# A two-layer streaming-encoder trunk on one Trainium2 core: late left operands kept on chip, and four re-ordered streams around the output product of layer 1

## The chip, the cores and the metric

The kernel runs on one core of a Trainium2 chip. A core has a matrix engine (PE, whose weight loads PEld overlap its matmuls), a vector engine (DVE), an activation engine (ACT), GpSimd (POOL) and SyncE (SP), and 16 DMA engines that all queues share. SP and POOL issue this kernel's DMAs here. The metric is the device time of one execution in microseconds (us).

## The reference

Two layers, each on x of 512 frames by 2048 features:

```python
h = rmsnorm(x, g_pre)
z = h @ w_in              # gq, gk, gv, gg, ga, aq, ak, av, ag
o_gla = gated linear attention over chunks of 64 frames, 4 heads (q, k: 128 wide, v: 256)
o_att = chunked softmax attention, 8 heads of 128, own chunk and 8 before it
o_gla = rmsnorm(o_gla, g_gla) * silu(gg);  o_att = rmsnorm(o_att, g_att) * silu(ag)
y = concatenate([o_gla, o_att]) @ w_out
x = x + rmsnorm(y, g_post)
```

Everything is float32; the result is x after the second layer.

## The kernel before

**The products.** Large products (w_in, w_out) are done on pairs of 512-column blocks by a seven-product scheme of Strassen's kind: P1, P5, P6, P3, P7, P2, P4, each a product of a sum of left blocks (S1 for P5, S2 for P6, S4 for P3, S3 for P7, A22 for P4) with a sum of weight blocks. A product is done in four chunks c of the contracted dimension, and one (product, chunk) is a **job**: 12 PE matmuls of 128x512, in fp32 precision built of a high and a low part of both operands: high weights `wh` against high left part, low weights `wl` against high left part, `wh` against low left part. A left operand is a tile of 128x1024 that holds high and low part (tags `sa`, `a...`, `g...`).

**What a job needs.** (1) `raw` (or `H`), 512 KB of weights, loaded by SP (L184, ring of four tiles); (2) for P5 and P6 a weight sum `H<-H,raw` on DVE (L250), for P7 a difference `raw<-H,raw` (L253); (3) the cast `wh` on ACT (L261); (4) the remainder `wl` on DVE (L267, ring of three); (5) the left operand, either resident, or brought back from device memory by SP (L238, in `bring`: `sa<-A`, `sa<-S`, `sa<-oS`).

**The part the change touches** is in layer 1, from about 1340 us on: the last input product (the value pair, GV), then the output product in two pairs of blocks, `W01` and `W23`. While PE does the value pair and the first output pair's P1 and P2, the gated-linear-attention half-heads are finished. `gla_line` runs them as units: outer products (L1300), states on DVE (L1320, L1322), read (PE, L1337), squares for the norm (ACT, L1347), gate (DVE, L1359), and `turn`: transposes on PE (L1370) and an eviction on ACT (L1381). `paired_sums` then makes S1, S2, S4 and S3 (DVE, L1512) and splits each into a high part (ACT cast, L113) and a low part (DVE, L114). The chunks come in the order 2, 3, 0, 1 (`C_END`); the sums of chunks 0 and 1 are the late ones, since they need the last units. S1 and S3 stay on chip. S2 and S4 are written to device memory (`oS`, POOL, L1526) and brought back by SP as `sa` when a job of P6 or P3 wants them, once for each output pair.

**Other streams around it.** `project` takes a finished output block from PE's bank: a sum of squares on ACT (L1598) and a product with the gains on DVE (L1601), the gains being loaded by POOL (L1588). `fetch_operands` (L1542) loads the attention half of the left operand (op_att, four tiles of 512 KB). `load_tokens` (L620) loads rows of the residual stream `x_mid` for the last sum; the half `xs1` is six loads, 2 MB.

**What sets the order.** Each engine works its instructions in order, and so does each DMA queue start its transfers. The order on each engine is set by the tile scheduler from a simulated timeline of the program; `tc.issue_after(x)` puts an instruction behind x, `delayed` and the pump of tasks say how many jobs on a task is called.

Of the kernel before, what the change touches and what calls it, by code (L numbers as in the profile page):

```python
# [35 lines left out]
def hybrid_trunk(  # L36
# [124 lines left out]
    last_evac = [None]  # L161
    last_out, last_put = [None], [None]
    last_cast, last_load, last_low, last_norm, last_state = [None], [None], [None], [None], [None]
# [14 lines left out]
    class Job:  # L178
# [39 lines left out]
        def bring(self):  # L218
# [5 lines left out]
            src = (so_d if end else sa_d)[self.l].get((name, c))  # L224
            if end and self.l in PAIRED and name in ("S1", "S3"):
                return
# [13 lines left out]
        def high(self):  # L240
            k, c, p = self.kind, self.c, self.pair
            if k == "std":
                src = self.raw
            else:
                h, r = p.get(("H", c)), p.get(("r", c))
                src = h if k in ("P1", "P5", "P6", "P4") and h is not None else r
                if k in ("P5", "P6") or k == "P4" and p["early"]:
                    opening = k == "P5" and self.b0 == W01[0]
                    with tc.issue_after(last_out[0]) if opening else nullcontext():
                        nc.vector.tensor_tensor(out=h, in0=h, in1=r, op=ALU.add)  # L250
                elif k == "P7":
                    with tc.issue_after(lows[-2]):
                        nc.vector.tensor_tensor(out=r, in0=h, in1=r, op=ALU.subtract)  # L253
# [170 lines left out]
    class Pair:  # L424
# [60 lines left out]
        def operand(self, job, k, c):  # L485
            if job.a is not None:
                return job.a
            if self.end and self.l in PAIRED and k in ("P5", "P7"):
                until(lambda: (LEFT[k], c) in A)
                return A[LEFT[k], c]  # L490
# [402 lines left out]
    def layer(l):  # L893
# [384 lines left out]
        class Unit:  # L1278
# [64 lines left out]
            def norm(self):  # L1343
                ss, self.r = sm(2), sm(2)
                for tt in range(2):
                    j = t2((256,), BF16)
                    nc.scalar.activation(  # L1347
                        j, self.ps_o[:, tt * 256 : (tt + 1) * 256], AF.Square, scale=256 ** -0.5,
                        accum_out=ss[:, tt : tt + 1],
                    )  # L1350
                if paired:
# [13 lines left out]
            def turn(self):  # L1365
# [13 lines left out]
                for f in range(2):  # L1379
                    kt = 2 * h + f  # L1380
                    nc.scalar.activation(  # L1381
                        full_o[:, f * 256 : (f + 1) * 256], ps[:, f * 256 : (f + 1) * 256], AF.Copy,
                        scale=gcol[:, l * 2 * KT + KT + kt : l * 2 * KT + KT + kt + 1],
                    )
                if paired and p:
# [43 lines left out]
        def gla_line():  # L1429
# [4 lines left out]
            while n < 8 or older is not None:  # L1434
# [25 lines left out]
                if older is not None:  # L1460
                    older.gate()
                    delayed.append([4 if newer is not None else 2, older.turn])
                yield
# [19 lines left out]
        def paired_sums():  # L1483
# [14 lines left out]
            while order:  # L1498
# [24 lines left out]
                if name in ("S1", "S3"):  # L1523
                    A[name, c] = z
                else:
                    last_put[0] = nc.gpsimd.dma_start(so_d[l][name, c], flat(z)).ins  # L1526
                made.add((l, True, name, c))
                yield
# [6 lines left out]
        def fetch_operands(k, c):  # L1535
            passed.add((k, c))
            for i in range(4):
                if ("P7", 1) in passed and 2 * i in heads_done and (0, i) not in op_att:
                    op_att[0, i] = slot(f"a11{i}", [2, 512], F32R)
# [102 lines left out]
        def paired_out():  # L1642
# [14 lines left out]
            def side(n):  # L1657
                def f(k, c):
# [10 lines left out]
                    elif (k, c) == ("P4", C_END[0]):  # L1669
                        gains[n] = load_gain(n, nc.gpsimd)  # L1670
                    if (n, k, c) in ((2, "P5", C_END[3]), (0, "P4", C_END[0])):
                        i = int(n == 0)
                        with tc.issue_after(last_put[0]):
                            held["xs", i] = load_tokens(i, x_src, nc.gpsimd)
                return f
# [141 lines left out]
```

## Time and profile before

| | us |
|---|---|
| median of 3 runs | 1617.53 (1614.9 to 1620.63) |
| the profiled execution's own time | 1618.17 |
| its span on the core | 1616.4 |
| PE busy in the span | 1584.1 (98%) |
| PEld | 1344.4 (83%) |
| DVE | 1274.6 (79%) |
| ACT | 931.7 (58%) |
| POOL | 172.2 (11%) |

A busy PE is not PE at its peak, since matmuls are pipelined and their ends modelled: one 128x512 matmul is listed with 0.39 us, but in an unbroken run the next one starts 0.227 us after it. So what PE loses is read from the rows in which it is idle and from the start times, not from its busy share. The same holds for DVE: a 128x1024 sum is listed with about 1.22 us, and the next instruction starts 1.14 us after it.

### The profile page before, as it was taken

To read this page: it belongs to the slowest core of one execution; us is meant where nothing else is said; L and a number is where in the kernel's file an instruction comes from. 1 tells how busy PE (TensorE), PEld (TensorE's weight loads), DVE (VectorE), ACT (ScalarE), POOL (GpSimd) and SP (SyncE) were. 2 spreads that over 40 slices of the span, in tenths; PEclk is the share of its full clock that TensorE was granted. 3 is DMA by queue.
4 is the path that set the end of the run, shared out by engine and by line. 5 is a ranking of instruction groups with operands and counts; after the bars stand their busy time and mean duration, and the time that the engine had idled before them with its cause. 6 is when DMAs were issued, how large, how long until landed. Compare 5 with 4: busy or idle time off the path is not lost.

```text
span 1616.4 us, 24395 instructions
## 1 busy us (share of the span) xinstructions
PE 1584.1 (98%) x8770; PEld 1344.4 (83%) x8770; DVE 1274.6 (79%) x1590; ACT 931.7 (58%) x1540; POOL 172.2 (11%) x300
## 2 busy tenths in 40 slices
PE   9999999999999999999999999999999999999897
PEld 5787889999988877788878888899999887677675
DVE  6878876877887876688859887868788767768788
ACT  8565544556686544555776555446667665456353
POOL 1131000001001101310121200000010010011101
PEclk9999999999999999999999999999999999999999
DMA  9999966858868697999778998768596757967795
GB/s 373 359 341 334 343 223 241 306 177 307 293 209 287 226 358 245 334 370 331 302 270 329 334 324 296 279 224 287 182 303 224 257 202 270 334 228 276 267 356 178
DMA packets 147753, 459.70 MB, mean 284 GB/s; under 512 B 16188, under 2 KB 35652, under 8 KB 147632
## 3 DMA queue, kind: packets, MB, share of 16 engines
q1 hardware_dynamic: 125936, 383.43, 67.2%
q0 software_dynamic: 21120, 73.76, 12.0%
q8 instruction: 69, 1.13, 0.3%
q10 hardware_dynamic: 576, 0.95, 0.2%
q14 instruction: 52, 0.43, 0.1%
HBM read 392.23 MB, written 64.77 MB: 283 GB/s over the span
## 4 chain that ended last, share of the span: by engine, by line
PE 88%; issue 4%; DVE 3%; DMA 3%; ACT 1%; POOL 0%; SPq 0%; POOLq 0%; DVEq 0%
PE mm L527 52%; PE mm L512 20%; PE mm L398 5%; PE ax L1128 2%; DMA raw<-in_w_dram 2%; DVE wl L267 1%; DMA H<-in_w_dram 1%; PE ax L1111 1%; PE ax L1300 1%; PE ax L1337 1%; DVE H L250 1%; PE ax L527 1%; PE ax L721 1%; PE ax L1090 1%; PE ax L1091 1%
## 5 line engine op out<-in xcount | busy, mean ns | idle before, releaser
L261 ACT CAST wh<-H 128x1024 fp32r<-128x1024 f32 x251 | 263.4, 1052 | 225.7 <-PE mm L527 93.2
L267 DVE TENSOR_TENSOR wl<-raw,wh 128x1024 fp32r<-128x1024 f32 x248 | 302.5, 1220 | 108.6 <-PE mm L527 37.2
L261 ACT CAST wh<-raw 128x1024 fp32r<-128x1024 f32 x248 | 260.9, 1053 | 212.7 <-PE mm L527 94.8
L267 DVE TENSOR_TENSOR wl<-H,wh 128x1024 fp32r<-128x1024 f32 (+1 forms) x253 | 307.2, 1217 | 86.0 <-PE mm L527 33.7
L527 PE MATMUL mm<-wh,sa 128*128 128x512 f32 x1088 | 347.6, 393 | 6.8 <-DMA sa<-oS 3.7
L527 PE MATMUL mm<-wh,g 128*128 128x512 f32 x928 | 289.6, 391 | 0.2 <-ACT mm L551 0.2
L527 PE MATMUL mm<-wh,a 128*128 128x512 f32 x864 | 278.3, 395 | 2.2 <-ACT a L113 1.1
L527 PEld LDWEIGHTS mm<-wh,sa 128*128 128x128 f32 x1088 | 203.2, 188 | 52.5 <-issue 5.2
L512 PE MATMUL mm<-sa,wh 128*128 128x256 f32 x1280 | 236.0, 285 | 0.0
L250 DVE TENSOR_TENSOR H<-H,raw 128x1024 f32<-128x1024 f32 x176 | 213.5, 1220 | 24.2 <-DMA raw<-in_w_dram 14.9
L527 PE MATMUL mm<-wl,sa 128*128 128x512 f32 x544 | 213.1, 392 | 0.1
L527 PEld LDWEIGHTS mm<-wh,g 128*128 128x128 f32 x928 | 174.9, 189 | 36.8 <-ACT mm L551 0.6
L512 PEld LDWEIGHTS mm<-sa,wh 128*128 128x128 f32 x1280 | 199.4, 192 | 0.3
L527 PEld LDWEIGHTS mm<-wh,a 128*128 128x128 f32 x864 | 161.2, 188 | 41.7 <-issue 5.0
L527 PE MATMUL mm<-wl,g 128*128 128x512 f32 x464 | 182.5, 393 | 6.1 <-DVE wl L267 5.9
L512 PE MATMUL mm<-sa,wl 128*128 128x256 f32 x640 | 180.8, 283 | 0.0
L527 PE MATMUL mm<-wl,a 128*128 128x512 f32 x432 | 169.8, 394 | 2.7 <-DVE wl L267 2.7
L512 PEld LDWEIGHTS mm<-sa,wl 128*128 128x128 f32 x640 | 122.3, 191 | 0.1
L527 PEld LDWEIGHTS mm<-wl,sa 128*128 128x128 f32 x544 | 102.2, 188 | 22.2 <-DVE wl L267 1.2
L527 PEld LDWEIGHTS mm<-wl,g 128*128 128x128 f32 x464 | 87.3, 188 | 29.1 <-DVE wl L267 11.2
L527 PEld LDWEIGHTS mm<-wl,a 128*128 128x128 f32 x432 | 81.2, 188 | 22.2 <-DVE wl L267 5.0
L512 PE MATMUL mm<-a,wh 128*128 128x256 f32 x512 | 94.5, 285 | 0.0
(227 smaller groups left out, 2016.3 us busy)
## 6 DMA issues: line engine op xcount, KB each, us to landing
raw<-in_w_dram SPq DMA_DIRECT2D x356, 512.0 KB, 5.3
sa<-S SPq DMA_DIRECT2D x128, 512.0 KB, 4.6
H<-in_w_dram SPq DMA_DIRECT2D x67, 512.0 KB, 6.0
S<-g POOLq DMA_DIRECT2D x32, 512.0 KB, 6.0
g<-S SPq DMA_DIRECT2D x32, 512.0 KB, 5.2
sa<-A SPq DMA_DIRECT2D x32, 512.0 KB, 6.1
sa<-oS SPq DMA_DIRECT2D x32, 512.0 KB, 5.4
oS<-g POOLq DMA_DIRECT2D x24, 512.0 KB, 5.9
```

The lines of the kernel that those rows point to most:

```text
L250: nc.vector.tensor_tensor(out=h, in0=h, in1=r, op=ALU.add)
L261: last_cast[0] = nc.scalar.copy(self.wh, src).ins
L267: last_low[0] = nc.vector.tensor_tensor(out=self.wl[:, kk, :], in0=self.src[:, kk, :], in1=self.wh[:, kk, :].bitcast(F32), op=ALU.subtract ...
L398: mm = nc.tensor.matmul(pss[o], a[:, part, t], rhs[:, kk, :], start=(i == 0 and kk == 0 and m == 0), stop=(i == n - 1 and kk == 1 and m == 2),
L512: nc.tensor.matmul(dst, lhs[:, kk, f], a[:, part, tok], start=(fresh and kk == 0 and m == 0 and ft % 2 == 0), stop=(c == self.last and kk ...
L527: mm = nc.tensor.matmul(out_ps[t], a[:, part, tok], rhs[:, kk, :], start=(fresh and kk == 0 and m == 0), stop=(c == self.last and kk == 1 ...
L721: mm = nc.tensor.matmul(gate_ps[l][g : g + 32, half * 256 : (half + 1) * 256], gate_w[l][:, kh * 8 + c * 2 + kk, :], full[half, c][:, kh, ...
L1090: nc.tensor.matmul(ps[:, :n], self.qh[:, t], self.kl[:, :n], start=False, stop=False)
L1091: nc.tensor.matmul(ps[:, :n], self.ql[:, t], self.kh[:, :n], start=False, stop=True)
L1111: nc.tensor.transpose(ps[:, j * P : (j + 1) * P], self.prob[i][:, j * P : (j + 1) * P], ident)
L1128: nc.tensor.matmul(o, self.pt[i][:, j * P : (j + 1) * P], av[hd // 4, j // 2][:, j % 2, (hd % 4) * P : (hd % 4 + 1) * P], start=(j == 0), ...
L1300: mm = nc.tensor.matmul(self.ps_u[cc][:, tt * 256 : (tt + 1) * 256], kd[p][r, tt, hk], self.gv[p][r, tt, hv], start=True, stop=True,).ins
```

## The change

All five parts act in layer 1 only. (1) The late S2 and S4 (chunks 0 and 1) stay on chip for the first output pair: `paired_sums` still writes them to device memory, since the second pair reads all eight from there, but `bring` returns and `operand` hands the tile itself to P6 and P3. (2) The rule that puts the weight sums of P5 behind `last_out` (the last L1601) holds for the late chunks alone, no longer for chunks 2 and 3. (3) The four op_att loads go to four places of the value pair (P5 chunk 3, P6 chunk 1, P6 chunk 3, P3 chunk 3) and no longer stand together at P7 chunk 1. (4) The newer half-head's squares (L1347) go in front of the older one's eviction (L1381), and the older one's `turn` is called 8 pump steps later and not 4. (5) The six loads of `xs1` are issued by SP without a rule, and no longer by POOL behind the last `oS` write.

```diff
--- before.py
+++ after.py
@@ -159,7 +159,7 @@
     HEAD = (("P1", 0), ("P1", 1), ("P2", 0), ("P2", 1), ("P1", 2), ("P2", 2))
     LEFT = {"P5": "S1", "P6": "S2", "P3": "S4", "P7": "S3", "P4": "A22"}
     last_evac = [None]
-    last_out, last_put = [None], [None]
+    last_out, last_put, last_square = [None], [None], [None]
     last_cast, last_load, last_low, last_norm, last_state = [None], [None], [None], [None], [None]
     made = set()
     lows, casts = [], []
@@ -222,7 +222,7 @@
             if self.a is not None:
                 return
             src = (so_d if end else sa_d)[self.l].get((name, c))
-            if end and self.l in PAIRED and name in ("S1", "S3"):
+            if end and self.l in PAIRED and (name in ("S1", "S3") or not p.get("second") and c in C_END[2:]):
                 return
             if src is None or p.get("direct") or p.get("second") and not end and (name, c) in RESIDENT:
                 return
@@ -245,7 +245,7 @@
                 h, r = p.get(("H", c)), p.get(("r", c))
                 src = h if k in ("P1", "P5", "P6", "P4") and h is not None else r
                 if k in ("P5", "P6") or k == "P4" and p["early"]:
-                    opening = k == "P5" and self.b0 == W01[0]
+                    opening = k == "P5" and self.b0 == W01[0] and c in C_END[2:]
                     with tc.issue_after(last_out[0]) if opening else nullcontext():
                         nc.vector.tensor_tensor(out=h, in0=h, in1=r, op=ALU.add)
                 elif k == "P7":
@@ -485,7 +485,7 @@
         def operand(self, job, k, c):
             if job.a is not None:
                 return job.a
-            if self.end and self.l in PAIRED and k in ("P5", "P7"):
+            if self.end and self.l in PAIRED and k in ("P5", "P6", "P3", "P7"):
                 until(lambda: (LEFT[k], c) in A)
                 return A[LEFT[k], c]
             if k in ("P1", "P2", "P4") and (self.l, LEFT.get(k), c) not in S_on:
@@ -1344,10 +1344,10 @@
                 ss, self.r = sm(2), sm(2)
                 for tt in range(2):
                     j = t2((256,), BF16)
-                    nc.scalar.activation(
+                    last_square[0] = nc.scalar.activation(
                         j, self.ps_o[:, tt * 256 : (tt + 1) * 256], AF.Square, scale=256 ** -0.5,
                         accum_out=ss[:, tt : tt + 1],
-                    )
+                    ).ins
                 if paired:
                     nc.gpsimd.tensor_scalar(out=ss, in0=ss, scalar1=EPS, scalar2=None, op0=ALU.add)
                     last_norm[0] = rsqrt(self.r, ss)
@@ -1378,10 +1378,11 @@
                 full_o = t2()
                 for f in range(2):
                     kt = 2 * h + f
-                    nc.scalar.activation(
-                        full_o[:, f * 256 : (f + 1) * 256], ps[:, f * 256 : (f + 1) * 256], AF.Copy,
-                        scale=gcol[:, l * 2 * KT + KT + kt : l * 2 * KT + KT + kt + 1],
-                    )
+                    with tc.issue_after(last_square[0]) if paired else nullcontext():
+                        nc.scalar.activation(
+                            full_o[:, f * 256 : (f + 1) * 256], ps[:, f * 256 : (f + 1) * 256], AF.Copy,
+                            scale=gcol[:, l * 2 * KT + KT + kt : l * 2 * KT + KT + kt + 1],
+                        )
                 if paired and p:
                     og_full[h] = full_o
                 else:
@@ -1459,7 +1460,7 @@
                     yield
                 if older is not None:
                     older.gate()
-                    delayed.append([4 if newer is not None else 2, older.turn])
+                    delayed.append([8 if newer is not None else 2, older.turn])
                 yield
                 yield
                 older = newer
@@ -1524,6 +1525,8 @@
                     A[name, c] = z
                 else:
                     last_put[0] = nc.gpsimd.dma_start(so_d[l][name, c], flat(z)).ins
+                    if c in late:
+                        A[name, c] = z
                 made.add((l, True, name, c))
                 yield
 
@@ -1535,7 +1538,8 @@
         def fetch_operands(k, c):
             passed.add((k, c))
             for i in range(4):
-                if ("P7", 1) in passed and 2 * i in heads_done and (0, i) not in op_att:
+                free = (("P5", 3), ("P6", 1), ("P6", 3), ("P3", 3))[len(op_att)] if paired and len(op_att) < 4 else ("P7", 1)
+                if free in passed and 2 * i in heads_done and (0, i) not in op_att:
                     op_att[0, i] = slot(f"a11{i}", [2, 512], F32R)
                     src = flat(turned[i][0]) if i == HEADS[-1] // 2 else oa_d[l][0, i]
                     with tc.issue_after(last_load[0]):
@@ -1668,10 +1672,11 @@
                         gains[n + 1] = load_gain(n + 1, nc.gpsimd)
                     elif (k, c) == ("P4", C_END[0]):
                         gains[n] = load_gain(n, nc.gpsimd)
-                    if (n, k, c) in ((2, "P5", C_END[3]), (0, "P4", C_END[0])):
-                        i = int(n == 0)
+                    if (n, k, c) == (2, "P5", C_END[3]):
                         with tc.issue_after(last_put[0]):
-                            held["xs", i] = load_tokens(i, x_src, nc.gpsimd)
+                            held["xs", 0] = load_tokens(0, x_src, nc.gpsimd)
+                    if (n, k, c) == (0, "P4", C_END[0]):
+                        held["xs", 1] = load_tokens(1, x_src, nc.sync)
                 return f
 
             until(lambda: all((0, i) in op_att or fetch_operands("end", 0) for i in range(4)))
```

The order that comes of it shows at three places; in the rows, the number behind a tile's name is its place in the program, and lines after the change count up to four higher (L1601 is then L1605, L1512 is L1513, L1478 is L1479, L1481 is L1482).

The first place is DVE where PE goes from P2 to P5 of the first output pair (wl_14774 is the first `wl` of P5, H_14357 its weight sum, H_14392, H_14431 and the last H those of the three further chunks). Before:

```order
L1601 TENSOR_TENSOR g_2949_14706<-mm_14374,t_2934_14628 128x512
L1601 TENSOR_TENSOR g_2952_14712<-mm_14375,t_2934_14628 128x512
L250 TENSOR_TENSOR H_14357<-H_14357,raw_14702 128x1024
L1512 TENSOR_TENSOR sa_14394<-sa_14394 128x512
L1512 TENSOR_TENSOR t_2897_14457<-a_2957_14735,t_2897_14457 128x512
L1512 TENSOR_TENSOR t_2907_14499<-a_2959_14740,t_2907_14499 128x512
L250 TENSOR_TENSOR H_14392<-H_14392,raw_14733 128x1024
L1512 TENSOR_TENSOR sa_14433<-sa_14433 128x512
L250 TENSOR_TENSOR H_14431<-H_14431,raw_14779 128x1024
L250 TENSOR_TENSOR H_14486<-H_14486,raw_14817 128x1024
L267 TENSOR_TENSOR wl_14774<-H_14357,wh_14731 128x1024
```

With the change:

```order
L250 TENSOR_TENSOR H_14357<-H_14357,raw_14702 128x1024
L267 TENSOR_TENSOR wl_14728<-raw_14684,wh_14700 128x1024
L1605 TENSOR_TENSOR g_2949_14706<-mm_14374,t_2934_14628 128x512
L1605 TENSOR_TENSOR g_2952_14712<-mm_14375,t_2934_14628 128x512
L1513 TENSOR_TENSOR sa_14394<-sa_14394 128x512
L1513 TENSOR_TENSOR t_2905_14489<-a_2957_14735,t_2905_14489 128x512
L1513 TENSOR_TENSOR t_2907_14499<-a_2959_14740,t_2907_14499 128x512
L1513 TENSOR_TENSOR sa_14433<-sa_14433 128x512
L250 TENSOR_TENSOR H_14392<-H_14392,raw_14733 128x1024
L267 TENSOR_TENSOR wl_14774<-H_14357,wh_14731 128x1024
```

H_14357 has moved ahead of both L1605 rows, and two of the four weight sums now come behind wl_14774; between the first L1605 and wl_14774 stand six instructions of 128x512 in both, but one weight sum where there were four.

The second place is SP's queue in the same stretch, ahead of P5's weights (raw_14702 is that of P5's first job). Before:

```order
L184 DMA raw_14622<-in_w_dram 128x1024
L1478 DMA a_2957_14735<-fa_176 128x2x256 x2
L184 DMA raw_14648<-in_w_dram 128x1024
L1481 DMA a_2958_14736<-fg_188 128x512
L184 DMA raw_14666<-in_w_dram 128x1024
L184 DMA raw_14684<-in_w_dram 128x1024
L184 DMA raw_14702<-in_w_dram 128x1024
L184 DMA raw_14733<-in_w_dram 128x1024
```

With the change:

```order
L184 DMA raw_14622<-in_w_dram 128x1024
L620 DMA g_3059_15223<-x_mid 128x1024
L1479 DMA a_2957_14735<-fa_176 128x2x256 x2
L184 DMA raw_14648<-in_w_dram 128x1024
L1482 DMA a_2958_14736<-fg_188 128x512
L620 DMA g_3060_15224<-x_mid 128x1024
L184 DMA raw_14666<-in_w_dram 128x1024
L620 DMA bias_15228<-x_mid 128x512
L184 DMA raw_14684<-in_w_dram 128x1024
L184 DMA raw_14702<-in_w_dram 128x1024
L620 DMA sg_15230<-x_mid 128x512
L184 DMA raw_14733<-in_w_dram 128x1024
```

Four of the six row loads now stand among the weight loads, three of them ahead of raw_14702; the other two stand just ahead of raw_14622.

The third place is DVE at the end of the value pair, at the states that the second half-head's read waits for (H_13473 is a weight sum of the same stretch, raw_14167 or raw_14156 its weights). Before:

```order
L267 TENSOR_TENSOR wl_14203<-H_13443,wh_14199 128x1024
L463 SCALAR_TENSOR_TENSOR g_2846_14212<-mm_13720,norm_210,ev_13873 128x512
L1320 COPY g_2816_14077<-ax_13709 128x256
L250 TENSOR_TENSOR H_13473<-H_13473,raw_14167 128x1024
L1322 SCALAR_TENSOR_TENSOR g_2816_14077<-g_2816_14077,a_end_8127,ax_13710 128x256
L1322 SCALAR_TENSOR_TENSOR g_2816_14077<-g_2816_14077,a_end_8127,ax_13709 128x256
```

With the change:

```order
L250 TENSOR_TENSOR H_13473<-H_13473,raw_14156 128x1024
L463 SCALAR_TENSOR_TENSOR g_2846_14212<-mm_13720,norm_210,ev_13873 128x512
L267 TENSOR_TENSOR wl_14203<-H_13443,wh_14199 128x1024
L1320 COPY g_2820_14085<-ax_13709 128x256
L1322 SCALAR_TENSOR_TENSOR g_2820_14085<-g_2820_14085,a_end_8127,ax_13710 128x256
L1322 SCALAR_TENSOR_TENSOR g_2820_14085<-g_2820_14085,a_end_8127,ax_13709 128x256
```

The weight sum, which waits for its weights, no longer stands between the states; on PE the read itself stands 14 matmuls later among the jobs than before.

## The prediction

> **What bounds the kernel now.** I began with the page's busy times: PE is the bound nearly everywhere.
>
> ```profile
> PE 1584.1 (98%) x8770; PEld 1344.4 (83%) x8770; DVE 1274.6 (79%) x1590; ACT 931.7 (58%) x1540; POOL 172.2 (11%) x300
> ```
>
> So only idle time of PE can be won. The table of what PE waits for, over the stretch from 1395 us to the end, names it (us in total, times, longest):
>
> ```profile
> PE mm L527 <- DVE wl L267: 6.7, 7, 3.3
> PE mm L527 <- DMA sa<-oS: 3.7, 2, 2.3
> PE mm L527 <- DMA sa<-A: 1.7, 1, 1.7
> PE ax L1337 <- DVE g L1322: 1.1, 1, 1.1
> PE mm L527 <- ACT ev L450: 0.9, 2, 0.7
> ```
>
> That is 14 us. Where the largest begins, PE's timeline shows:
>
> ```profile
> 1474.28 0.39 PE L527 MATMUL mm<-wl,a 128*128 128x512 f32 x1
> ...
> 1474.96 0.39 PE L527 MATMUL mm<-wl,a 128*128 128x512 f32 x1
> ...
> 1477.45 0.61 PE L527 MATMUL mm<-wh,g 128*128 128x512 f32 x2
> 1481.34 0.50 PE L527 MATMUL mm<-wl,g 128*128 128x512 f32 x1 [3.28 <-DVE wl L267]
> ```
>
> Three matmuls take 0.68 us, so one takes 0.227 and a job of twelve 2.72 us. At 1477.45 PE enters P5 of the first output pair and stands for 3.28 us. The windows of the next stretches tell whose work that is (columns: us, PE, PEld, DVE, ACT, POOL busy, PE clock, DMA share, GB/s):
>
> ```profile
> 1477.00:1500.00 23.00, 18.15 (x69) 13.52 (x68) 23.00 (x29) 15.81 (x25) 0.31 (x1) 0.93 0.45 165
> 1482.00:1486.00 4.00, 3.96 (x11) 2.62 (x9) 4.00 (x7) 2.93 (x5) 0.00 (x0) 0.57 0.90 362
> ```
>
> DVE is busy for all 23 us of P5, PE is not; behind the 3.28 us wait the clock was 0.57 for 4 us. P5 is bound by DVE, and DVE's timeline shows its order:
>
> ```profile
> 1469.29 1.23 DVE L267 TENSOR_TENSOR wl<-raw,wh 128x1024 fp32r<-128x1024 f32 x1 [1.94 <-PE mm L527]
> ...
> 1471.93 1.28 DVE L1601 TENSOR_TENSOR g<-mm,t 128x512 f32<-128x512 f32 x2
> 1473.12 1.21 DVE L250 TENSOR_TENSOR H<-H,raw 128x1024 f32<-128x1024 f32 x1
> 1474.26 0.68 DVE L1512 TENSOR_TENSOR sa<-sa 128x512 f32<-128x512 f32 x1
> 1474.86 1.28 DVE L1512 TENSOR_TENSOR t<-a,t 128x512 f32<-128x512 f32 x2
> 1476.06 1.22 DVE L250 TENSOR_TENSOR H<-H,raw 128x1024 f32<-128x1024 f32 x1
> 1477.20 0.68 DVE L1512 TENSOR_TENSOR sa<-sa 128x512 f32<-128x512 f32 x1
> 1477.80 2.35 DVE L250 TENSOR_TENSOR H<-H,raw 128x1024 f32<-128x1024 f32 x2
> 1480.07 1.21 DVE L267 TENSOR_TENSOR wl<-H,wh 128x1024 fp32r<-128x1024 f32 x1
> ...
> 1495.24 1.21 DVE L267 TENSOR_TENSOR wl<-H,wh 128x1024 fp32r<-128x1024 f32 x1
> ```
>
> Start to start, a 128x1024 instruction costs 1.14 us (2.27 for the two at 1477.80) and one of 128x512 0.60. From T = 1471.93, the first L1601, to the first remainder of P5 are 9.3 us; four of the eleven instructions are weight sums.
>
> **Late S2 and S4 on chip (part 1).** POOL's and SP's timelines and the chain of waits show the reload:
>
> ```profile
> 1503.17 1.13 POOL L1526 DMA_DIRECT2D oS<-g  x2 [1.20 <-DVE g L114]
> 1504.54 1.05 POOL L620 DMA_DIRECT2D g<-x_mid  x2 [0.24 <-issue]
> ...
> 1506.67 1.11 POOL L620 DMA_DIRECT2D sg<-x_mid  x2
> ```
>
> ```profile
> 1503.77 1.58 SPq L238 DMA_DIRECT2D sa<-oS  x2
> 1505.44 1.84 SPq L184 DMA_DIRECT2D raw<-in_w_dram  x1
> ```
>
> ```profile
> 1505.44 10.93 DMA raw<-in_w_dram
> ```
>
> Everything comes at once from 1503 to 1507: reloads, 2 MB of rows and weights, and the weights take 10.93 us to land. With the operand read where it was made, the 3.7 us of `sa<-oS` go whole, and with the rows gone too the late weights (0.9 us of the `wl` waits, at 1518.81) should land in time. All of it lies on the path, since PE goes on with P6 and P3 at once; the cover that is left is DVE, worked out next, which makes the late operands' low parts in time by its order.
>
> **P5's sums (part 2), and the new path.** I walked the changed DVE order from T, the first L1605, with 0.60 and 1.14. To the first remainder of P5: six small and two large, 3.6+2.28 = 5.9 us, 3.4 less than now. To the second: four small, three large, 11.7. The third: six and two, 17.6. The fourth: one and two, 20.5. The first of P6: one large, 21.6; now that ends at T+24.5 (1495.24+1.14). The first of P3: five small and three large more, 28.0. P5's fourth job leaves PE at about T+22.7 and P6's first at T+25.4, so PE waits some 2 us for P3's first remainder at T+28.0; every later one is ahead of PE. From there 128 matmuls are left to the end of P7, 29.0 us: **P7 ends at T+57.0**. Now P4 begins at
>
> ```profile
> 1536.32 0.50 PE L527 MATMUL mm<-wh,g 128*128 128x512 f32 x1 [0.20 <-ACT mm L551]
> ```
>
> with P7's last at 1535.7, or T+63.8. So on one and the same T the change is worth 6.8 us: 2.9 from DVE's order and the rest from the late operands and weights.
>
> On the clock: the 3.28 us wait above was followed by 0.57. The changed chain has waits of some 3 us between the P5 jobs (5.8 us of DVE against 2.72 of PE). A job at half rate would take 5.4 us, less than the 5.8 that DVE needs for the next one, so I price it at 0. [...]
>
> **What T will be.** T is the latest of three. (a) The `wl` ring: the row at 1469.29 waited 1.94 us for PE; PE comes earlier by the upstream gain, worked out below as 2.0, so wl_14728 ends at 1468.4 and T could be 1468.4. (b) The gains on POOL's queue and (c) raw_14702, H_14357 and then wl_14728 behind it:
>
> ```profile
> t<-in_g_post_dram POOLq DMA_DIRECT2D x2, 256.0 KB, 8.7
> ```
>
> ```profile
> DMA to landing us min/median/max: 3.2/4.3/7.9
> ```
>
> ```profile
> 1456.27 11.44 SPq L184 DMA_DIRECT2D raw<-in_w_dram  x5
> ```
>
> (the last two: weight loads of 1450 to 1475). The gains land about 8.7 us after an issue near 1463, at 1471.3, so T by (b) is 1469.3 to 1471.3. raw_14702 is the third of the five; issued near 1462, it lands 5 to 7.9 us later, up to 1469.9. In the changed kernel it is asked for 2.0 us earlier, but behind the rows.
>
> **Rows on SyncE (part 5).** 2 MB leave 1504 to 1507 and go to 1436 to 1465, where the windows show:
>
> ```profile
> 1430.00:1440.00 10.00, 10.00 (x48) 7.18 (x45) 5.93 (x12) 4.77 (x10) 0.92 (x2) 1.00 0.41 145
> 1440.00:1450.00 10.00, 10.00 (x53) 7.48 (x53) 7.01 (x10) 6.55 (x13) 0.92 (x2) 1.00 0.22 69
> ...
> 1460.00:1470.00 10.00, 10.00 (x48) 8.29 (x47) 6.25 (x8) 5.25 (x9) 4.05 (x6) 1.00 1.02 364
> ```
>
> About half falls in the idle stretch and costs nothing; 1 MB falls near 1460, where the engines are full, and at 364 GB/s costs 2.9 us, ahead of raw_14702. It then lands at 1467.9 to 1470.8 (1462, 2.0 earlier, 5 to 7.9 and 2.9 later), and with 1.14 each for H_14357 and wl_14728 T is 1470.2 to 1473.1. I take **T = 1472.0**, above the middle, as full engines show the late end. Then P5 ends no earlier than now: the upstream gain is spent waiting for DVE.
>
> [...]
>
> **Upstream: op_att (3) and squares (4).** SP's timeline at the end of the value pair and PE's two waits:
>
> ```profile
> 1395.08 0.99 SPq L1542 DMA_DIRECT2D a<-oa  x2
> 1396.12 0.42 SPq L238 DMA_DIRECT2D sa<-A  x1
> ```
>
> ```profile
> 1405.06 0.47 PE L527 MATMUL mm<-wh,sa 128*128 128x512 f32 x1 [1.73 <-DMA sa<-A]
> 1411.48 1.08 PE L1337 MATMUL ax<-g,g 128*64 128x256 f32 x8 [1.14 <-DVE g L1322]
> ```
>
> Two op_att loads stand right ahead of the operand that PE waits 1.73 us for. Moved up, the same bytes delay an earlier operand: 0.9 of 1.73 is taken as won (bounds 0 and 1.73). The read stands 14 matmuls (3.2 us) later and no weight sum stands among its states: 1.14 won (bounds 0 and 1.14). Sum 2.0, bounds 0 to 2.9; it counts only by way of T. The squares' new place has no wait of its own in the table: 0, covered by an ACT that is busy for 58%.
>
> **The sum.** P7 ends at 1472.0+57.0 = 1529.0 and not 1535.7: 6.7 us. What follows is unchanged, so the profiled time 1618.17 becomes 1611.5. The median before is 0.64 below that time, within its three runs' spread of 5.7; I leave the 1611.5.
>
> **The rivals.** (A) T slips to about 1475: the rows weigh on the weights with all their 2 MB, or nothing is won upstream. For it: the share of 1.02 at 1460. Against it: the 0.22 before it. P7 ends at 1532.0, 3.7 us won: **1614.5**. (B) T falls to 1469.3, rows hidden whole, gains early: against it are the 8.7 us that gains take. P7 ends at 1526.3, 9.4 won: **1608.8**, and with the late remainders a little earlier 1608. (C) Slower: SP works in order, and the last row load (into the tile `sg`) waits until the last half-head's gate tile has been transposed on PE and its old reads are over, with raw_14733 and all later weights behind it. raw_14733's sum has about 4 us of room: asked for near 1464.5 now, with 7.9 at most to land, and summed at 1476.06. Each us held beyond that is a us of T; from about 11 us of holding (4 of room and 6.7 of gain) the change loses, and at 16 us the time is **1623**. Against it: the transposes stand about 17 us ahead of P5 in PE's order, so the tile should be free when its turn comes. (D) Part 1 saves nothing, since the reload is hidden once the rows have left its way: then late remainders on DVE bind P6, and the time is (A)'s, in whose chance I put it.
>
> **How the numbers follow.** Forecast 0.45 (1609 to 1613.5), (A) with (D) 0.26, (B) 0.17, (C) 0.12. A change of 0.3%, 4.9 us, is about what a measurement of this kernel can tell from none, so faster means under 1612.7: of the forecast's 0.45 some 0.37, and all of (B): 0.54. Same: 0.08 of the forecast and all of (A): 0.34. Slower: (C), 0.12. The range runs from 1606.5, under (B), to 1618, over (A); it leaves out (C) and a few tails.
>
> **What would show it.** Right: no `sa<-oS` wait after 1500, DVE at 10.00 through P5, the first `wl` of P5 5.9 us behind the first L1605, P3's first wait of some 2 us. Wrong: T before 1470 or after 1474, a DVE that idles in P5 (then a load or PE sets the pace, and the walk along DVE is void), a stall at an earlier operand of the value pair above 2 us, or SP standing for over 4 us at a row load.

## The result, and the profile after

The changed kernel takes 1609.91 us (median of four runs, 1608.8 to 1611.06), the kernel before 1618.36 in the same series (1614.9 to 1620.63): a ratio of 0.995, 95% interval 0.9929 to 0.997, 8.4 us by the medians. The forecast was 1611.5. A later series gave 0.9955 (0.994 to 0.997) for the same kernel; the kernel before had medians of 1618.0 to 1619.0 in the three later ones.

The profiled execution took 1608.8 us, its span is 1607.0. What PE waits for from 1390 us on, with the change:

```profile
PE mm L527 <- DVE wl L267: 7.1, 5, 2.9
PE mm L527 <- ACT mm L457: 0.9, 1, 0.9
PE mm L527 <- ACT wh L261: 0.5, 1, 0.5
```

The waits for `sa<-oS`, `sa<-A` and the states are gone; what is left is DVE's. DVE's timeline at the start of P5:

```profile
1463.16 1.22 DVE L267 TENSOR_TENSOR wl<-raw,wh 128x1024 fp32r<-128x1024 f32 x1 [0.26 <-PE mm L527]
1469.84 1.23 DVE L250 TENSOR_TENSOR H<-H,raw 128x1024 f32<-128x1024 f32 x1 [5.45 <-DMA raw<-in_w_dram]
1470.98 1.22 DVE L267 TENSOR_TENSOR wl<-raw,wh 128x1024 fp32r<-128x1024 f32 x1
1472.12 1.28 DVE L1605 TENSOR_TENSOR g<-mm,t 128x512 f32<-128x512 f32 x2
...
1476.86 1.22 DVE L267 TENSOR_TENSOR wl<-H,wh 128x1024 fp32r<-128x1024 f32 x1
...
1498.97 1.22 DVE L267 TENSOR_TENSOR wl<-raw,wh 128x1024 fp32r<-128x1024 f32 x1
```

T, the first product with the gains, is 1472.12 (forecast 1472.0); the first `wl` of P5 is done 5.9 us behind it, P3's first 28.0 us, both as walked. The surprise is the second row: DVE stands 5.45 us for one weight load, raw_14702, with a remainder and both products with the gains queued behind the sum that waits. SP's timeline shows the row loads on both sides of it (raw_14702 is the second of the two `raw` loads):

```profile
1452.91 0.38 SPq L620 DMA_DIRECT2D bias<-x_mid  x1
1457.59 3.24 SPq L184 DMA_DIRECT2D raw<-in_w_dram  x2
1460.92 1.47 SPq L620 DMA_DIRECT2D sg<-x_mid  x1
```

The last row load found its tile nearly free (1.47 us on the queue), so nothing was held for long, as rival (C) would have it. PE's timeline, at P5's first job, at P3's and where P4 begins:

```profile
1474.66 0.61 PE L527 MATMUL mm<-wh,g 128*128 128x512 f32 x2
1478.13 0.74 PE L527 MATMUL mm<-wl,g 128*128 128x512 f32 x1 [2.85 <-DVE wl L267]
```

```profile
1500.24 0.50 PE L527 MATMUL mm<-wl,sa 128*128 128x512 f32 x1 [1.82 <-DVE wl L267]
```

```profile
1529.40 0.39 PE L527 MATMUL mm<-wh,g 128*128 128x512 f32 x1
```

PE comes to P5 2.8 us earlier than before (1474.66 and 1477.45) and waits there. P4 begins 6.9 us earlier (1536.32 before), and from there to the end of the span it is 77.6 us where it was 80.1.

### The profile page after: what moved, and what is told of

Same layout as the page of the kernel before. It is cut to its first block, busy times and chain, and to the rows that moved or that the text cites. A ratio compares the mean times of both kernels' runs of the same rounds, so it can differ in the third digit from the quotient of the medians.

```text
span 1607.0 us, 24384 instructions
## 1 busy us (share of the span) xinstructions
PE 1581.4 (98%) x8770; PEld 1346.3 (84%) x8770; DVE 1274.9 (79%) x1590; ACT 933.2 (58%) x1540; POOL 173.9 (11%) x294
## 4 chain that ended last, share of the span: by engine, by line
PE 89%; DMA 3%; issue 3%; DVE 3%; ACT 1%; POOL 1%; SPq 0%; POOLq 0%; DVEq 0%; ACTq 0%
PE mm L527 53%; PE mm L512 20%; PE mm L398 6%; PE ax L1128 2%; DMA raw<-in_w_dram 2%; PE ax L1111 1%; PE ax L1300 1%; PE ax L1337 1%; DVE wl L267 1%; DMA H<-in_w_dram 1%; PE ax L527 1%; PE ax L721 1%; PE ax L1090 1%; PE ax L1091 1%; PE ax L1089 1%
## 5 line engine op out<-in xcount | busy, mean ns | idle before, releaser
L527 PE MATMUL mm<-wh,sa 128*128 128x512 f32 x1056 | 336.1, 393 | 2.0 <-ACT mm L457 0.9
L527 PE MATMUL mm<-wh,g 128*128 128x512 f32 x960 | 299.4, 391 | 0.0
L527 PEld LDWEIGHTS mm<-wh,sa 128*128 128x128 f32 x1056 | 197.3, 188 | 45.6 <-issue 1.8
L527 PEld LDWEIGHTS mm<-wh,g 128*128 128x128 f32 x960 | 180.9, 188 | 37.6
L527 PE MATMUL mm<-wl,sa 128*128 128x512 f32 x528 | 206.9, 392 | 1.8 <-DVE wl L267 1.8
L527 PE MATMUL mm<-wl,g 128*128 128x512 f32 x480 | 188.5, 393 | 5.2 <-DVE wl L267 5.2
L527 PEld LDWEIGHTS mm<-wl,g 128*128 128x128 f32 x480 | 90.6, 189 | 26.8 <-DVE wl L267 8.0
```

Source lines behind the costliest of these rows:

```text
L527: mm = nc.tensor.matmul(out_ps[t], a[:, part, tok], rhs[:, kk, :], start=(fresh and kk == 0 and m == 0), stop=(c == self.last and kk == 1 ...
```

## The experiments

Times of whole runs mostly lie within some 2 us of their median, single ones up to 5.7 above it, and the profiled spans contain up to 4.3 us that arise ahead of every edit: PE's 7401st matmul, up to which all the kernels are alike, starts at 1295.8 us in the changed kernel's first profile and at 1300.1 in its second. So I read three stretches from each trace: from that matmul to T, from T to the start of P4, and from there to the end. "Median" is that of the timed runs, the ratio is to the kernel before in the same series.

| kernel | median us | ratio (95%) | to T | T to P4 | P4 to end |
|---|---|---|---|---|---|
| before | 1618.0 to 1619.0 | 1 | 175.8 | 64.4 | 80.1 |
| changed | 1609.91 | 0.995 (0.9929 to 0.997) | 176.3 | 57.3 | 77.6 |
| changed, again | 1610.14 | 0.9955 (0.994 to 0.997) | 176.0 | 57.3 | 79.5 |
| before + part 1 | 1610.59 | 0.9953 (0.9939 to 0.9966) | 174.2 | 56.9 | 80.7 |
| before + parts 3, 4 | 1615.72 | 0.9987 (0.9977 to 0.9997) | 172.3 | 65.3 | 79.6 |
| changed - part 1 | 1613.11 | 0.9963 (0.9951 to 0.9975) | 176.3 | 58.9 | 79.6 |
| changed - part 2 | 1609.65 | 0.9942 (0.993 to 0.9954) | 173.5 | 58.4 | 77.6 |
| changed - part 3 | 1609.69 | 0.9951 (0.9938 to 0.9965) | 174.0 | 59.3 | 77.8 |
| changed - part 4 | 1611.60 | 0.9963 (0.995 to 0.9976) | 180.3 | 52.0 | 79.0 |
| changed - part 5 | 1609.93 | 0.9949 (0.9935 to 0.9962) | 175.0 | 58.9 | 80.5 |
| changed, rows behind P6's loads | 1610.76 | 0.995 (0.9937 to 0.9962) | 174.1 | 58.9 | 78.1 |
| changed, P6's late sums later | 1610.01 | 0.9952 (0.9939 to 0.9966) | 175.9 | 55.8 | 78.9 |
| both | 1608.21 | 0.9942 (0.9931 to 0.9954) | 174.9 | 55.8 | 78.3 |
| both, and - part 2 | 1605.71 | 0.9923 (0.9909 to 0.9937) | 171.4 | 56.1 | 78.5 |

**The changed kernel without part 1.**

```diff
-            if end and self.l in PAIRED and (name in ("S1", "S3") or not p.get("second") and c in C_END[2:]):
+            if end and self.l in PAIRED and name in ("S1", "S3"):
...
-            if self.end and self.l in PAIRED and k in ("P5", "P6", "P3", "P7"):
+            if self.end and self.l in PAIRED and k in ("P5", "P7"):
...
-                    if c in late:
-                        A[name, c] = z
```

> The changed kernel without part 1: the late S2 and S4 are brought back from device memory again. Theory of the prediction (the reload is a wait of its own): two waits of some 3.7 us in all for sa<-oS return after 1500 us, and the time is about 3.7 us above the changed kernel's 1609.9, near 1613.6. Rival (the reload is hidden once the rows have left its way): no such wait above 0.5 us, and the time within 1 us of 1609.9.

Measured: 1613.11, as the theory had it, but not for its reason. PE's waits from 1500 us on:

```profile
PE mm L527 <- DVE wl L267: 3.4, 3, 1.8
```

No operand is waited for: with the rows gone from POOL's queue, the reload of the late S2 and S4 lands in time. The rival was right about the wait and wrong about the time. Of the 3.2 us the trace shows 1.6 between T and P4, as a half clock behind PE's wait at P3 (us, busy PE, PEld, DVE, ACT, POOL, clock, DMA share, GB/s; the second row is the same window of the changed kernel):

```profile
1504.00:1508.00 4.00, 4.00 (x15) 3.11 (x14) 2.00 (x2) 1.04 (x1) 0.00 (x0) 0.71 0.87 293
```

```profile
1504.00:1508.00 4.00, 4.00 (x19) 3.32 (x18) 2.02 (x2) 1.05 (x1) 0.00 (x0) 1.00 0.91 322
```

The rest would be remainders late after P4, 0 to 2 us by the two profiles of the changed kernel; how much of that is the 2 MB of reloads is not settled. Nor is the half clock shown to be the reloads' doing: the changed kernel with the rows moved has part 1 and shows it at the same place (0.57 from 1498 to 1502 us, below).

**The kernel before with part 1 alone** (the inverse of that diff, on the kernel before).

> The kernel before with part 1 alone: late S2 and S4 kept on chip for the first pair. Theory of the prediction: the two waits for sa<-oS (3.7 us) go and PE comes so much earlier to P7; 4 us less than before. Rival, from the run without part 1 (no such wait returned, yet 3.2 us): the four reloads cost by the 2 MB they add to the queue that brings the weights; then the rows, which stay on POOL here, still hold the weights of P3 and P7 back, the wait moves from the operand to wl, and 1 to 2 us are won.

Measured: 1610.59, 7.9 us won: twice what the theory gave it, and neither it nor the rival. DVE's order at P5 is that of the kernel before, four weight sums ahead of the first `wl`:

```profile
1470.91 1.29 DVE L1603 TENSOR_TENSOR g<-mm,t 128x512 f32<-128x512 f32 x2 [0.25 <-DMA t<-in_g_post_dram]
1472.12 1.21 DVE L250 TENSOR_TENSOR H<-H,raw 128x1024 f32<-128x1024 f32 x1
...
1476.79 2.35 DVE L250 TENSOR_TENSOR H<-H,raw 128x1024 f32<-128x1024 f32 x2
1479.06 1.22 DVE L267 TENSOR_TENSOR wl<-H,wh 128x1024 fp32r<-128x1024 f32 x1
```

```profile
1527.78 0.39 PE L527 MATMUL mm<-wh,g 128*128 128x512 f32 x1
```

The first `wl` starts 8.2 us behind T, and yet P4 begins 56.9 us behind T, no later than with the whole change (57.3). After P6's first remainder, which in the old order is done 24.5 us behind T, PE waits for nothing from 1496 us on until P4; the new order has P6's first at 21.6 and then makes PE wait for P3's first at 28.0. The old order has P3's first two small instructions and itself behind P6's, 26.8 us behind T, and no wait there. So the new order gives P5 what it takes from P3.

**The kernel before with parts 3 and 4 alone**, to see the order apart. These two, not part 2, put two of P5's weight sums behind the first `wl`, as the run's trace shows (below: one sum at 1470.25 and one at 1473.80 stand ahead of it).

```diff
-                if ("P7", 1) in passed and 2 * i in heads_done and (0, i) not in op_att:
+                free = (("P5", 3), ("P6", 1), ("P6", 3), ("P3", 3))[len(op_att)] if paired and len(op_att) < 4 else ("P7", 1)
+                if free in passed and 2 * i in heads_done and (0, i) not in op_att:
...
+                    with tc.issue_after(last_square[0]) if paired else nullcontext():
...
-                    delayed.append([4 if newer is not None else 2, older.turn])
+                    delayed.append([8 if newer is not None else 2, older.turn])
```

> The kernel before with parts 3 and 4 alone, which by the listing of the order are what puts two of P5's weight sums behind its first wl on DVE. Theory (the order on DVE is worth its instructions, whichever part made it): first wl of P5 some 7.0 us behind the first product with the gains and not 9.3, 2 to 3 us less than before. Rival (P6 and P3 still wait for the reload of the late operands, which is not sooner): PE only waits longer for sa<-oS, and less than 1 us is won.

```profile
1468.98 1.29 DVE L1603 TENSOR_TENSOR g<-mm,t 128x512 f32<-128x512 f32 x2 [0.90 <-DMA t<-in_g_post_dram]
1470.25 1.22 DVE L250 TENSOR_TENSOR H<-H,raw 128x1024 f32<-128x1024 f32 x1
...
1473.80 1.22 DVE L250 TENSOR_TENSOR H<-H,raw 128x1024 f32<-128x1024 f32 x1
1474.94 1.22 DVE L267 TENSOR_TENSOR wl<-H,wh 128x1024 fp32r<-128x1024 f32 x1
```

```profile
1512.36 0.76 PE L527 MATMUL mm<-wh,sa 128*128 128x512 f32 x1 [5.37 <-DMA sa<-oS]
```

Both were half right. The first `wl` is done 7.1 us behind T and T comes 3.5 us earlier, but the reload now takes one wait of 5.37 us where there were 3.7, and T to P4 is 65.3 us, not shorter than 64.4. What is won, 0.13% (0.03 to 0.23%), goes with the earlier T; from T to P4 nothing is won. Here the wait for the reload bounds that stretch, so this run cannot tell what the order is worth once that wait is gone. With part 1 in place the stretch is 56.9 us in the old order and 57.3 in the changed kernel.

**The changed kernel without part 5** (rows on POOL behind the last `oS` write again):

```diff
-                        held["xs", 1] = load_tokens(1, x_src, nc.sync)
+                        with tc.issue_after(last_put[0]):
+                            held["xs", 1] = load_tokens(1, x_src, nc.gpsimd)
```

> The changed kernel without part 5: the six row loads are issued by POOL again, behind the last oS write. Theory (rows ahead of the weights on SyncE set T, the first product with the gains): the weights of P5's first job land some 2.5 us earlier, T falls from 1472.1 to about 1469.5, and the rows delay the weights of P7 and P4 instead, which gives 2 to 4 us back as waits for wl after 1500: time 1609 to 1612. Rival (rows cost nothing where they are now, and much where they were): T stays at 1472, waits of 2 to 4 us after 1500, time 1612 to 1614.

Measured: 1609.93, no difference. T is 1.3 us earlier (175.0), half of what was expected. In the profile the last stretch is 80.5 us, with remainders awaited until 1545, 1591 and 1596, as if part 5 moved a cost from one place to the other. That is not shown: the profiled execution was the slowest of its six (1615.23), and the last stretch of the changed kernel itself varies by 1.9 us.

**The changed kernel without part 2.**

```diff
-                    opening = k == "P5" and self.b0 == W01[0] and c in C_END[2:]
+                    opening = k == "P5" and self.b0 == W01[0]
```

> The changed kernel without part 2: all four weight sums of P5 behind the last product with the gains again; on DVE only H_14357 moves, from ahead of wl_14728 to behind the two products with the gains. Theory of the prediction (one weight sum taken off the chain behind T is worth its 1.14 us): time 1.1 us above 1609.9, near 1611. Rival, from the trace of the changed kernel (DVE stands 5.45 us for the weights of H_14357, with wl_14728 and two products with the gains held behind it): these three, 2.3 us, go into the wait, the first wl of P5 ends at about 1475.7 and not at 1478.0, and the time is 2.3 us lower, near 1607.6.

Measured: 1609.65, not to be told from 1609.91. In the trace wl_14728 goes into the wait, as the rival said; the products with the gains then wait for the gains:

```profile
1469.62 1.23 DVE L267 TENSOR_TENSOR wl<-raw,wh 128x1024 fp32r<-128x1024 f32 x1 [1.10 <-PE mm L527]
1473.42 1.29 DVE L1605 TENSOR_TENSOR g<-mm,t 128x512 f32<-128x512 f32 x2 [2.57 <-DMA t<-in_g_post_dram]
1474.62 1.22 DVE L250 TENSOR_TENSOR H<-H,raw 128x1024 f32<-128x1024 f32 x1
```

T falls by 2.8 us, 1.1 of it given back since the weight sum is on the chain again. Part 2 is worth nothing here, and its place ahead of an awaited load costs it.

**The changed kernel without part 3, and without part 4.**

```diff
-                free = (("P5", 3), ("P6", 1), ("P6", 3), ("P3", 3))[len(op_att)] if paired and len(op_att) < 4 else ("P7", 1)
+                free = ("P7", 1)
```

> The changed kernel without part 3: the four op_att loads together at P7 chunk 1 of the value pair again. Theory (what is won ahead of P5 is spent waiting for DVE there): a wait of about 1.7 us for sa<-A returns near 1405 us, PE's wait at the start of P5 shrinks by as much, and the time stays within 1 us of 1609.9. Rival (the upstream gain reaches the end, by way of T): 1.7 us more, 1611.6.

```diff
-                    with tc.issue_after(last_square[0]) if paired else nullcontext():
+                    with nullcontext():
...
-                    delayed.append([8 if newer is not None else 2, older.turn])
+                    delayed.append([4 if newer is not None else 2, older.turn])
```

> The changed kernel without part 4: the older half-head's eviction in front of the newer one's squares again, its transposes 4 pump steps earlier. Theory: a wait of about 1.1 us at a read near 1411 us returns if this part was what moved it, PE's wait at P5 shrinks by as much, time within 1 us of 1609.9. Rival (this part also sets when the last half-heads are done, and so when the late sums stand in DVE's order): the chain from T to P3's first remainder is longer than 28.0 us, and the time is 2 us or more higher.

Without part 3: 1609.69, as the theory had it, though no wait for `sa<-A` came back in this profile. T was 2.0 to 2.4 us earlier (174.0), and from T to P4 it was 2.0 us longer (59.3 and 57.3). Without part 4: 1611.6 (1609.64 to 1613.28), inside the spread. There the products with the gains come late, behind the first two remainders of P5 (T 180.3), PE waits 3.8 us for them ahead of P5, and P4 still begins where it does with the change (232.3 us from the common matmul; 233.3 and 233.6). Neither the theory's wait at a read nor the rival's longer chain showed.

**The rows later, and P6's late sums later.** Two edits on the changed kernel against the two waits its trace still shows: the rows behind P6's last weight load (on SP at 1481 to 1484 us), and P6's weight sums of the late chunks behind P3's first remainder.

```diff
                 p["r", c] = self.fetch(rtile("raw"), b1, bottom)
+                if self.l in PAIRED and b0 == W01[0] and c == C_END[3]:
+                    row_gate[0] = last_load[0]
...
-                        held["xs", 1] = load_tokens(1, x_src, nc.sync)
+                        with tc.issue_after(row_gate[0]):
+                            held["xs", 1] = load_tokens(1, x_src, nc.sync)
```

> The changed kernel with the six row loads still on SyncE, but behind the last weight load of P6, where the DMA share was 0.13 to 0.7 (1485 to 1500 us). Theory (rows ahead of P5's weights set T): the 5.45 us wait of H_14357 shrinks by 2 to 3 us, T falls to about 1469.5, and the time is 2 to 3 us lower, 1607 to 1608. Rival (T is set by the gains on POOL's queue or by the ring of wl, or the rows now hold the weights of P7): no gain, 1609.5 to 1612.

```diff
-                    with tc.issue_after(last_out[0]) if opening else nullcontext():
+                    late6 = k == "P6" and self.b0 == W01[0] and self.l in PAIRED and c in C_END[2:]
+                    with tc.issue_after(last_out[0]) if opening else tc.issue_after(lows[-3]) if late6 else nullcontext():
```

> The changed kernel, with P6's weight sums of the two late chunks (first output pair) put behind the remainder of P3's first job on DVE. Theory (after P5 the time follows DVE's order): that remainder ends 25.7 us and not 28.0 us behind the first product with the gains, PE's wait of 1.8 us at P3's first job goes, and with it the chance of half a clock behind it: 2 to 3 us lower, 1607 to 1608. Rival (another wait takes its place: the postponed sums are late for P6's third job): a new wait of 1.5 us or more some 8 to 12 us later, 1609 to 1611.

The rows alone: 1610.76, no gain, as the rival had it. T did fall by 2.2 us, but PE then waited as long at P3's first job, and in this profile a half clock followed it there:

```profile
1498.00:1502.00 4.00, 3.71 (x9) 2.96 (x10) 3.71 (x5) 0.00 (x0) 1.07 (x2) 0.57 0.79 300
```

The sums alone: 1610.01, no gain in the time either; the wait at P3 did go and T to P4 fell to 55.8, 1.5 us less, and the last stretch was 78.9 against 77.6 and 79.5. The new wait that the rival named did not come either (0.2 us at P3's second job). The theory's 2 to 3 us were missed; why the time does not show the 1.5 us is open.

**Both together, and both without part 2.**

> The changed kernel with both: the rows behind P6's last weight load and P6's late sums behind P3's first remainder. Theory: T earlier by 2.2 us as measured in the run with the rows moved, no wait at P3's first job and so nothing there that puts the clock down: 4 to 5 us lower than the changed kernel, 1605 to 1606. Rival (what T gains is lost again to the clock or to weights held behind the rows, as in the run with the rows alone): no better than the run with the sums alone, 1607 to 1609.

> The changed kernel with the rows behind P6's last weight load, P6's late sums behind P3's first remainder, and part 2 undone (H_14357 behind the two products with the gains). Theory (what stands 2.3 us behind the awaited weight sum can go into its wait, as the run without part 2 showed in its trace): 1 to 2 us less than the same without that, 1606.5 to 1607.5. Rival (the products with the gains then wait for the gains themselves): 1608 to 1609.

Both: 1608.21 (1607.88 to 1608.76), in the rival's range but better than the sums alone; T was earlier by only 1.1 to 1.5 us, going by the two profiles of the changed kernel. Both and part 2 undone: 1605.71 (1603.92 to 1607.49), below what even the theory gave it, beside 1610.14 (1608.9 to 1615.87) for the changed kernel in that series: this version beats both kernels. DVE's timeline and PE's waits after 1500:

```profile
1466.97 1.22 DVE L270 TENSOR_TENSOR wl<-raw,wh 128x1024 fp32r<-128x1024 f32 x1 [1.10 <-PE mm L530]
1468.47 1.29 DVE L1608 TENSOR_TENSOR g<-mm,t 128x512 f32<-128x512 f32 x2 [0.27 <-DMA t<-in_g_post_dram]
1469.67 1.22 DVE L253 TENSOR_TENSOR H<-H,raw 128x1024 f32<-128x1024 f32 x1
```

```profile
PE mm L530 <- DVE wl L270: 0.6, 2, 0.3
```

Nothing on DVE waits for weights there any more, T is 4.6 to 5.0 us earlier than in the changed kernel's two profiles, and of PE's waits from 1500 on 0.6 us are left.

**The changed kernel again.**

> The changed kernel as it is, beside the three others on one chip: 1609 to 1611, against which they are read. A second profile of it also shows whether the half clock behind PE's wait at P3's first job, seen in three of the other profiles and not in the first of this kernel, comes and goes with one and the same order: then it shows in some profiles only; if the order decides it, it stays away here.

Measured: 1610.14, in the range. The half clock stayed away from P3 in this profile too (1.00 from 1490 to 1560 us), while it shows behind PE's wait there without part 1 (0.71 from 1504 to 1508 us) and with the rows moved (0.57 from 1498 to 1502 us); two profiles of one order do not show whether the order decides it. The last stretch did change with one and the same kernel: 77.6 us in the first profile, 79.5 in the second, with remainders awaited until 1590 and 1596.

## Why the prediction was right, and where it was not

The time, 1609.91 for 1611.5, was right, and so was the path. **The walk** along DVE's order held at every point: 5.9, 11.7, 17.6, 20.4 and 28.0 us behind T for the remainders walked, a wait of 1.82 us at P3 for "some 2", and P4 at T+57.3, where the walk has P7 end at T+57.0. **T** was 1472.12 for 1472.0, set by raw_14702 behind the rows, as argued; (a) and (b) were not the bound. That it met to a tenth of a us is luck, since the terms under it were off and made up for one another. The rows were priced at 2.9 us; T fell by 2.2 with them behind P6's loads and by 1.3 with them on POOL, and DVE still stood 3.26 and 3.96 us for the weights there. Rival (A)'s 1475 is an estimate, 2.9 us for the other 1 MB at the 364 GB/s of 1460 to 1470 us; no run shows it, and what the rows cost T in the two runs that moved them is the 2.2 and 1.3 us. (In (b), 8.7 us behind 1463 is 1471.7 and not 1471.3; nothing rests on it.)

**The split of the gain was wrong.** The prediction said of the 6.8 us from T to P4: "2.9 from DVE's order and the rest from the late operands and weights". The run with part 1 alone has the old order, and the rows still on POOL, and 56.9 us: once the late operands stay on chip, the order adds nothing on this path. The prediction gave late operands and weights 3.9 us together; in that run they bring 7.5. Counted from T, PE there is level with the kernel before until 102 matmuls ahead of P4 (33.8 us in both). It gains 4.0 us where the two waits for `sa<-oS` stood, and 3.5 more behind them, where the kernel before waits for evictions and for late remainders (0.7 us at 1518.81 and 0.9 at 1533.56; the prediction read 0.9 at the first). So without the reloads the weights were in time although the rows had not moved.

Part 1 is not the only way there: without it, but with the other four, T to P4 is 58.9 us, 1.6 of it the half clock. With parts 3 and 4 alone it is 65.3.

The step that failed compared the two orders at P6's first remainder (21.6 and 24.5) and took the difference for a gain at the end, though the same walk had just found a new wait for P3's first remainder at 28.0; in the old order that one is done at 26.8. The 2.9 us are back before P3. The 6.8 itself is a little small: it sets the end of the walk against the start of P7's last matmul (1535.7); against the start of P4 (1536.32) the walk gives 7.4, and 7.1 were measured.

**The cause of the order was wrong too.** The prediction put the new order under part 2. The runs with parts 3 and 4 alone and without part 2, both with two weight sums between T and the first `wl`, show that it comes from parts 3 and 4; part 2 only moved one sum ahead of T, into the wait for its weights.

**(D)** was right about the wait (without part 1 none for `sa<-oS` comes back once the rows are on SP) and not about the time, 3.2 us, of which the profile puts 1.6 down to the half clock. Part 1 removes that wait, and so do the other four together; that among them it is part 5, which moves the rows, is likely but not shown, since part 5 alone on the kernel before was not run. Without part 1 the four bring 5.9 us (1618.96 to 1613.11). On the kernel before, part 1 alone does it and brings 7.9 of some 8.4 us, and no one of the other four, taken out, moves the time by more than the spread.

**Upstream**, 2.0 were expected; P5's start is 2.8 us earlier (1477.45 to 1474.66), of which 0.3 lie ahead of every edit, so 2.5, and 2.8 by the second profile. In the first, another 0.7 us are idle for wl_14728 just ahead of it: the stall that I moved to an earlier operand did not appear. It was swallowed at T, as forecast: from the common matmul T is 176.3 and 176.0, before 175.8.

**After P4** the prediction left all unchanged. The first profile has 2.4 us less there, the second about half a us: that would cover the 1.6 us by which the forecast was too high, and it varies from execution to execution.

**The half clock** was priced at 0 in P5, and that held: behind the 2.85 us wait it ran at half rate (0.50 from 1478.21 to 1481.62 us), and the next `wl` came later still: PE waited 1.20 us for it, up to 1483.94. That P3's wait could bring it too, as it did without part 1 (0.71 from 1504 to 1508 us), where PE is the bound, was overlooked.

## What to carry to other kernels

Walk the dependent engine's order to the end of the stretch, under both orders, before a gain at one instruction is booked: what an order gives one consumer it may take from the next. An instruction that waits for a transfer should not stand ahead of ready work on its engine (here DVE stood 5.45 us, and undoing part 2 beside the two other edits won 2.5 us by the medians), and bulk loads that nobody needs soon belong behind the loads that somebody waits for, in the queue as well as in time (T fell by 2.2 us). Where several waits lay close behind one another, taking one away showed nothing (1610.76 and 1610.01 us beside 1609.91); where two parts remove the same wait, taking one out understates it (part 1: 3.2 us taken out, 7.9 alone); the two edits that each gave nothing here gave about 2 us together (a difference that the intervals do not quite carry) and 4.4 with a third (which they do).

## What was not expected of the hardware

PE's clock went to half behind gaps well under 3.28 us. Without part 1 it followed PE's wait of 1.8 us at P3's first job: it set in 1.5 us after the wait and lasted some 3.4 us (eight starts 0.43 apart and not 0.23, 1.6 us lost). The 3.41 us ahead of it, and the half clock itself (columns as above):

```profile
1499.53:1502.94 3.41, 1.63 (x7) 1.24 (x7) 3.41 (x5) 0.36 (x1) 1.01 (x3) 1.00 0.89 318
1502.94:1506.35 3.41, 3.41 (x9) 2.64 (x8) 3.06 (x3) 1.04 (x1) 0.48 (x1) 0.50 0.91 255
```

With the rows moved it set in at once behind the wait there (0.57 from 1498 to 1502 us, 0.76 from 1500 to 1504, 1.00 from 1504 on to 1508). In the changed kernel, with a wait of 1.8 us at the same place and, in the first profile, 2.2 us between the two matmul starts (1498.04 and 1500.24), it did not come in either profile: the clock was 1.00 from 1490 to 1560 us in both.

Behind P5's first wait it came in both kernels. In the kernel before it ran from 1482.39 to 1485.80 us (0.50), 1.1 us after the 3.28 us wait; in the changed kernel's first profile from 1478.21 to 1481.62, 0.1 us after the 2.85 us wait. Yet a later gap of the kernel before, 2.69 us between the starts at 1511.24 and 1513.93 (a 2.30 us wait for `sa<-oS`), had no half clock behind it (1.00 from 1511 to 1600 us), though it is longer than the one at P3's first job.

So the length of a gap alone does not decide in these profiles, and what does decide is not shown.
